# Moving all query and key projections of a hybrid encoder step ahead of its linear attention, by way of a DRAM scratch

## The chip, the core and the metric

The kernel runs on one core of a Trainium2 chip. A core has TensorE (PE in the profile; its weight loads are listed apart as PEld), VectorE (DVE), ScalarE (ACT), GpSimd (POOL) and SyncE (SP), which here issues every DMA. The metric is the device time of one execution in microseconds, as the median of several runs.

## What is computed

The reference is one layer of an encoder step, for a prompt of 1024 frames (8 tiles of 128) and 32 sample frames of a running stream. All arithmetic is fp32.

```
xn = rmsnorm(x);  u = xn @ w_in            # 1024 x (11 groups of columns)
gq, gk, gv, gr, gg, dq, dk, dv, dg, ma, mb = split(u)
dq, dk = rope(dq), rope(dk)                # first 16 of every 64 channels
o_gla  = gated linear attention, 4 heads, chunk by chunk (a running state)
for each of 8 heads of differential attention:
    p1 = softmax(q1 k1^T / 8), p2 = softmax(q2 k2^T / 8)   # block-causal mask
    o_diff = (p1 - lam * p2) @ v
merged = sigmoid(ma) * (yg @ w_proj_gla) + sigmoid(mb) * (yd @ w_proj_diff)
y = x + rmsnorm(merged @ w_out)            # yg, yd: normed, times silu(gg), silu(dg)
```

The rotated keys and the values are outputs as well. The sample's 32 frames attend to 512 cached keys and to themselves.

## The kernel before

Every fp32 matrix product is done as three products of split operands: a rounded high part and the rest, high x high, low x high, high x low. So each weight tile and each activation has a high and a low half, made by a copy on ACT and a subtraction on DVE or POOL.

A **projection block** is one 128-column slice of a weight matrix against all 1056 frames: 3 chunks of 352 frames x 8 slices of the inner dimension x 3 products = 72 matmuls. `wtile` (line 422) loads its 512 KB of weights, rounds them on ACT (line 426) and subtracts on POOL (line 428). `proj` (line 431) runs a block in one go; `fill` (line 441) runs a list of blocks in pieces of two inner slices, to be woven between other work.

The stages, in order:

1. normalisation of the input, and the values of both attentions (lines 326 to 415);
2. gated linear attention (GLA, lines 481 to 752): per head `gla_prep` makes the decay factors and the scaled q and k, `gla_head` walks over nine chunks with a running state;
3. differential attention (lines 754 to 1048): `diff_main` takes eight heads one behind the other, and in each head eight query blocks; `sample_thread` does the sample frames;
4. the output projections of GLA (`pg_first`), of the differential heads, and the final product with `w_out`.

In stages 2 and 3 the order of PE's instructions is written out by a planner, the class `Order` (line 62). It keeps a modelled clock, the banks of PSUM in use and a table `W` of assumed latencies. Several generators offer their next step with a cost and the events that it needs; the planner takes the first one in the list that is ready. The attention threads stand first, the projection blocks of `fill` last, so blocks go where the attention threads are waiting by the plan. The other engines are ordered by the scheduler of the language, with a higher priority for `diff_main`. PE then executes its instructions in this fixed order, whatever the real latencies are.

The list of blocks decides what there is to weave in. In stage 2 it is, head after head, two silu gate blocks of the head before, q and k, and then as many **gate blocks** (the sigmoid gates ma and mb, 16 in all, stored to DRAM) as `GATES_GLA` says: [0, 1, 1, 1, 1]. A silu block of head h needs head h-1 to be finished, a q block the previous head's `if`, a k block the previous head's transposed keys. In stage 3 each head h has the rotated query block and the rotated key block of head h+1, its own silu block `dgate_job` (which needs the end of head h-1), and gate blocks by `GATES_DIFF`: [2, 1, 1, 1, 1, 1, 1, 2, 2], the first entry ahead of head 0. The names "dq", "dk" in `W` are the latencies that the planner assumes from the end of such a block to usable operands.

The rotated blocks are where the change lies. `rot_job` (line 784) evacuates a block into `rr` (line 799), swaps eight rows at a time by four small DMAs into `sw` (lines 791 and 792), multiplies `sw` with the sines on POOL (line 793), multiplies and adds on DVE (lines 795 and 797), and calls `split_q` (line 802) or `split_k` (line 818). These write the high and low halves of the two sub-heads; for matmuls over 128 rows each sub-head's 64 rows must stand twice, and for the keys four DMAs copy 64 rows to the other 64 (line 832). The key tiles k0, k1, kl0, kl1 have one buffer each, the query tiles two.

`diff_main` (line 895) emits, for a head, the scores of block 0 (`diff_scores`, line 864), the closing steps of the previous head (`diff_fin`), the load of the head's values into a buffer `sg1` (line 903), which in stage 2 held the silu gate, and then for each i the scores of block i+1, the transposes of block i (line 926) and, after every second block, the product with the values (lines 939 to 941). The scores of the next head come behind all this.

## Time and profile before

| | |
|---|---|
| median of 3 runs | 1517.67 us (1513.35 to 1520.35) |
| the profiled execution | 1523.35 us, span 1521.6 us |
| mean granted TensorE clock | 0.981 |
| DMA | 152.29 MB, mean 100 GB/s |
| stage 2 on PE | about 222 to 551 us |
| first scores of differential attention | 601.8 us |
| first output projection | 1220.7 us |

The profile is of one execution. Per group of instructions it gives the source line, engine, operation, tiles, count, busy time, mean duration, and the idle time of the engine just before them with what ended it. PE's matmuls are pipelined: the duration of one (some 320 ns for 352 columns) is longer than the distance to the next (some 160 ns), so for PE the useful measure is how many start in a stretch. Further views are the chain of waits that ended last, the waits, the busy time by stretch of time and the timeline.

### The profile page before, as it was taken

The page shows a single profiled execution, that of the slowest core. Times are in us where ns is not written, and L with a number is a line of the kernel's source. Part 1 is how long each engine was busy: PE and PEld are TensorE (multiplying, and loading weights), DVE is VectorE, ACT ScalarE, POOL GpSimd, SP SyncE. Part 2 cuts the span into 40 slices and gives each one's busy share as a digit, 9 for nine tenths or more (in the row PEclk, how much of TensorE's full clock was granted, in tenths as well). Part 3 has the DMA queues.
Part 4 walks back from the last instruction along what each step waited for, and adds up shares of the span by engine and source line. Part 5 has one row for each costly group of instructions (what it writes and reads, how often), then busy time and mean ns, then how long its engine had stood idle before and what let it go on. Part 6 is the DMA issues. An engine that isn't in the chain of part 4 may idle for free.

```text
span 1521.6 us, 22330 instructions
## 1 busy us (share of the span) xinstructions
PE 1438.6 (95%) x8848; PEld 1340.6 (88%) x8848; DVE 792.0 (52%) x1464; ACT 623.2 (41%) x1282; POOL 298.4 (20%) x186
## 2 busy tenths in 40 slices
PE   8999999989999998998999998989899999999997
PEld 6787789889989898998989897989798889999997
DVE  5602005655474343757685866677764544155415
ACT  4603114635353323564655564555555443022311
POOL 1200002222222233121222222212221112122001
PEclk9999999999999999999999998999999999999999
DMA  8621111221222144131323132223212187433305
GB/s 294 205 104 37 44 48 43 61 85 56 89 70 78 58 145 130 46 88 60 102 75 88 60 102 76 74 73 88 89 50 89 67 271 248 168 130 117 109 1 187
DMA packets 66118, 152.29 MB, mean 100 GB/s; under 512 B 9920, under 2 KB 28480, under 8 KB 65488
## 3 DMA queue, kind: packets, MB, share of 16 engines
q1 hardware_dynamic: 66000, 150.71, 30.9%
q8 instruction: 74, 1.21, 0.3%
q14 instruction: 44, 0.36, 0.1%
HBM read 100.16 MB, written 39.98 MB: 92 GB/s over the span
## 4 chain that ended last, share of the span: by engine, by line
PE 51%; DVE 7%; ACT 4%; DMA 2%; issue 1%; POOL 1%; SPq 0%; DVEq 0%; POOLq 0%; ACTq 0%
PE ps_w L458 9%; PE ps_w L459 9%; PE ps_w L460 9%; PE ps_w L437 2%; PE ps_w L436 2%; PE ps_w L438 2%; PE ps_c L1176 2%; PE ps_c L1174 2%; PE ps_c L1175 2%; PE ps_t L926 2%; PE ps_s L879 2%; PE ps_s L878 2%; DVE p L888 1%; DMA kl<-kl 1%; PE po L940 1%
## 5 line engine op out<-in xcount | busy, mean ns | idle before, releaser
L458 PE MATMUL ps_w<-X,wh 128*128 128x352 f32 x1344 | 455.2, 339 | 7.5 <-ACT k L489 3.2
L459 PE MATMUL ps_w<-X,wl 128*128 128x352 f32 x1344 | 440.2, 328 | 0.0
L460 PE MATMUL ps_w<-X,wh 128*128 128x352 f32 x1344 | 438.3, 326 | 0.0
L428 POOL TENSOR_TENSOR wl<-wr,wh 128x1024 fp32r<-128x1024 f32 x72 | 178.5, 2479 | 688.5 <-ACT wh L426 551.2
L458 PEld LDWEIGHTS ps_w<-X,wh 128*128 128x128 f32 x1344 | 257.9, 192 | 12.5 <-DVE sg L471 4.0
L459 PEld LDWEIGHTS ps_w<-X,wl 128*128 128x128 f32 x1344 | 257.9, 192 | 1.2 <-issue 1.2
L460 PEld LDWEIGHTS ps_w<-X,wh 128*128 128x128 f32 x1344 | 258.5, 192 | 0.0
L884 ACT ACTIVATE p<-ps_s,nm 128x256 f32<-128x256 f32 (+7 forms) x128 | 94.4, 740 | 60.8 <-DVE nm L882 35.9
L426 ACT ACTIVATE wh<-wr 128x1024 fp32r<-128x1024 f32 x72 | 75.9, 1054 | 61.0 <-PE ps_w L460 35.7
L283 PE MATMUL ps_v<-wh,X 128*128 128x512 f32 x248 | 97.6, 394 | 1.4 <-DVE X L222 1.4
L282 PE MATMUL ps_v<-wh,X 128*128 128x512 f32 x248 | 98.3, 397 | 0.0
L284 PE MATMUL ps_v<-wl,X 128*128 128x512 f32 x248 | 98.2, 396 | 0.0
L882 DVE TENSOR_REDUCE nm<-ps_s 128x1 f32<-128x256 f32 (+7 forms) x128 | 95.0, 746 | 2.7
L880 DVE MEMSET ps_s<- 64x64 f32 x128 | 14.3, 112 | 118.4 <-PE ps_s L879 116.9
L269 DVE TENSOR_TENSOR vo<-ps_v,vo 32x512 f32<-32x512 f32 x4 | 2.7, 679 | 140.7 <-ACT vo L268 140.7
L926 PE MATMUL ps_t<-ident,p 128*128 128x128 f32 x288 | 49.0, 280 | 25.6 <-DVE ps_s L880 13.8
L928 ACT ACTIVATE ah<-ps_t 128x512 fp32r<-128x512 f32 (+2 forms) x96 | 46.8, 488 | 58.5 <-PE ps_t L926 57.8
L878 PE MATMUL ps_s<-k,q 128*128 128x512 f32 (+2 forms) x192 | 69.3, 368 | 1.2 <-DMA k<-k 1.2
L879 PE MATMUL ps_s<-kl,q 128*128 128x512 f32 (+2 forms) x192 | 65.0, 354 | 4.0 <-DMA kl<-kl 3.8
L643 POOL TENSOR_TENSOR vl<-vr,vh 128x512 fp32r<-128x512 f32 (+1 forms) x20 | 24.8, 1238 | 223.2 <-ACT vh L642 223.2
L265 ACT ACTIVATE vo<-ps_v 128x512 f32<-128x512 f32 x32 | 19.0, 595 | 114.9 <-PE ps_v L284 114.5
L926 PEld LDWEIGHTS ps_t<-ident,p 128*128 128x128 f32 x288 | 35.9, 143 | 32.8 <-issue 22.5
(318 smaller groups left out, 3039.3 us busy)
## 6 DMA issues: line engine op xcount, KB each, us to landing
wr<-w SPq DMA_DIRECT2D x72, 512.0 KB
thd<-gate SPq DMA_DIRECT2D x16, 528.0 KB
xn<-xn SPq DMA_DIRECT2D x16, 512.0 KB
wr<-wv SPq DMA_DIRECT2D x16, 512.0 KB
newk<-rr SPq DMA_DIRECT2D x8, 528.0 KB
ygr<-ygd SPq DMA_DIRECT2D x8, 528.0 KB
tha<-thd SPq DMA_DIRECT2D x8, 528.0 KB
ydr<-ydd SPq DMA_DIRECT2D x8, 528.0 KB
```

What stands on the lines that cost most here:

```text
L282: mm(ps, xk[:, 0, t0 : t0 + P], wh[:, k, :], start=(k == 0), stop=False)
L283: mm(ps, xk[:, 1, t0 : t0 + P], wh[:, k, :], start=False, stop=False)
L284: mm(ps, xk[:, 0, t0 : t0 + P], wl[:, k, :], start=False, stop=(k == KT - 1))
L428: nc.gpsimd.tensor_tensor(wl, wr, wh.bitcast(F32), op=ALU.subtract)
L458: mm(ps[:, :n], wh[:, k, :], src[k][:, 0, t0 : t0 + n], start=(k == 0), stop=False)
L459: mm(ps[:, :n], wl[:, k, :], src[k][:, 0, t0 : t0 + n], start=False, stop=False)
L460: mm(ps[:, :n], wh[:, k, :], src[k][:, 1, t0 : t0 + n], start=False, stop=(k == KT - 1))
L878: mm(ps[:, n0 : n0 + n], qs[m][:, qsl], ks[m][:, n0 : n0 + n], start=True, stop=False)
L879: mm(ps[:, n0 : n0 + n], qs[m][:, qsl], kls[m][:, n0 : n0 + n], start=False, stop=True)
L882: ve.tensor_reduce(nm, ps[:, 0:w], axis=AX.X, op=ALU.max, negate=True)
L884: act(p[:, 0:w], ps[:, 0:w], AF.Exp, bias=nm, accum_out=sm[:, m : m + 1])
L926: nc.tensor.transpose(ps[:, (j - j0) * P : (j - j0 + 1) * P], p[:, j * P : j * P + P], ident)
```

## The change

All 16 query and key blocks of differential attention, and two gate blocks, run in a dense stage of their own, behind the values and before GLA. Their raw results go to two flat DRAM scratch tensors `qd` and `kd`, the queries already scaled. Rotation is done for four heads at a time: the 8 + 8 rotated rows of four heads' sub-heads are gathered from the scratch into one 128-row tile, turned there by three DVE operations and stored back. GLA has no gate blocks any more; differential attention has 14 gate blocks and no rotated blocks. Each head's operands are loaded from the scratch in `diff_main` of the head before, at query blocks 1, 3 and 5: each sub-head's rows are loaded twice and then split in place. Keys have two buffers. Weights of the new stage have three raw buffers.

```diff
-GATES_GLA = [0, 1, 1, 1, 1]
-GATES_DIFF = [2, 1, 1, 1, 1, 1, 1, 2, 2]
+GATES_GLA = [0, 0, 0, 0, 0]
+GATES_DIFF = [2, 2, 2, 2, 2, 1, 1, 1, 1]
-N = {"fin": 1, "rr": 3, "q": 2, "k": 4, "fill": 2, "first": 200, "evac": 1200, "lead": 2}
+N = {"fin": 1, "rr": 3, "q": 2, "k": 2, "fill": 2, "first": 200, "evac": 1200, "lead": 2}
...
-    "dq": 7.76, "dk": 14.32,
+    "dq": 16.0, "dk": 16.0,
...
+    qd = dram.tile([D, T], F32, name="qd")
+    kd = dram.tile([D, T], F32, name="kd")
...
+    def turn(d, g, new):
+        part = lambda s: d.rearrange("(a c) t -> a c t", c=HD)[g * 8 : g * 8 + 8, s * 8 : s * 8 + 8, :]
+        r = rq.tile([P, T], F32, tag="r", name="r")
+        sw = rq.tile([P, T], F32, tag="sw", name="sw")
+        for s in range(2):
+            dma(r[s * HD : s * HD + HD], part(s))
+            dma(sw[s * HD : s * HD + HD], part(1 - s))
+        ve.tensor_tensor(sw, sw, stb, op=ALU.mult)
+        ve.tensor_tensor(r, r, ct, op=ALU.mult)
+        ve.tensor_tensor(r, r, sw, op=ALU.add)
+        for s in range(2):
+            st(part(s), r[s * HD : s * HD + HD])
+            if new is not None:
+                for h in range(4):
+                    o = r[s * HD + h * 16 : s * HD + h * 16 + 16]
+                    st(new[4 * g + h].rearrange("(m d) t -> m d t", m=2)[:, s * 8 : s * 8 + 8, :], o)
+
+    def qk_block(b, d, h, scale, new):
+        r = rq.tile([P, T], F32, tag="nat", bufs=3, name="nat")
+        proj(wtile(b + h, rq, 3), xs, lambda ps, sl: act(r[:, sl], ps, AF.Copy, scale=scale))
+        st(d[h * P : h * P + P], r)
+        if new is not None:
+            for m in range(2):
+                st(new[h, m * HD + 16 : m * HD + HD, :], r[m * HD + 16 : m * HD + HD])
+    late = ()
+    for g in range(2):
+        for b, d, scale, new in ((BLK_DK, kd, 1.0, a["newk"]), (BLK_DQ, qd, SC, None)):
+            for h in range(4 * g, 4 * g + 4):
+                qk_block(b, d, h, scale, new)
+                if h == 4 * g and late:
+                    turn(*late)
+            late = d, g, new
+    for n in range(2):
+        b, event, begin, _ = gate_job(*gates.pop(0))
+        evac, done = begin()
+        proj(wtile(b, rq, 3), xs, evac)
+        done()
+        if n == 0:
+            turn(*late)
+    rq.release()
...
+    def fetch_rows(t, d, h, m):
+        for half in (0, HD):
+            dma(t[half : half + HD], d[(2 * h + m) * HD : (2 * h + m + 1) * HD, 0:NP])
+    def fetch_k(h):
+        kls = [dp.tile([P, NP], F32R, tag=f"kl{m}", bufs=2, name=f"kl{m}") for m in range(2)]
+        for m in range(2):
+            fetch_rows(kls[m].bitcast(F32), kd, h, m)
...
+    def split_k(h):
+        for m in range(2):
+            kl = dks[h][1][m]
+            kh = dp.tile([P, NP], F32R, tag=f"k{m}", bufs=2, name=f"k{m}")
+            for c in parts(NP, N["k"]):
+                act(kh[:, c], kl[:, c].bitcast(F32), AF.Copy)
+                ve.tensor_tensor(kl[:, c], kl[:, c].bitcast(F32), kh[:, c].bitcast(F32), op=ALU.subtract)
...
+    def fetch_q(h, m):
+        raw = tp.tile([P, NP], F32, tag="sg1", name="qraw")
+        fetch_rows(raw, qd, h, m)
+        return raw
+    def split_q(h, m, raw):
+        q = dp.tile([P, NP], F32R, tag=f"q{m}", bufs=2, name=f"q{m}")
+        for c in parts(NP, N["q"]):
+            act(q[:, c], raw[:, c], AF.Copy)
+            ve.tensor_tensor(q[64:128, c], raw[64:128, c], q[64:128, c].bitcast(F32), op=ALU.subtract)
...
+    def head_ahead(h, i, raw):
+        if i == 1:
+            fetch_k(h)
+            return fetch_q(h, 0)
+        if i == 3:
+            split_k(h)
+            split_q(h, 0, raw)
+            return fetch_q(h, 1)
+        if i == 5:
+            split_q(h, 1, raw)
+            return fetch_v(h)
+        return raw
...
+                if h + 1 < DH:
+                    raw = head_ahead(h + 1, i, raw)
                 if i + 1 < NQ:
                     yield from diff_scores(h, i + 1, att)
...
+    raw0 = None
+    for i in (1, 3, 5):
+        raw0 = head_ahead(0, i, raw0)
```

Removed are `rot_job`, the old `split_q` and `split_k`, their rope tables and swap tile, and the load of the values at the start of a head.

## The prediction

> **What bounds the kernel now.** I read the page first: its busy shares.

> ```profile
> span 1521.6 us, 22330 instructions
> PE 1438.6 (95%) x8848; PEld 1340.6 (88%) x8848; DVE 792.0 (52%) x1464; ACT 623.2 (41%) x1282; POOL 298.4 (20%) x186
> ```

> PE is busy 95% of the span, no other engine more than 52%. So time can leave only through PE's holes, or through less matmul work. The change removes no matmul. It moves whole projection blocks between stages, so the question is where PE will have something to do. Next I asked for the busy time by stretch (columns: window, length, busy us and count of PE, PEld, DVE, ACT, POOL, clock, DMA share, GB/s): gated linear attention (GLA), the wait for the first head, and the eight heads.

> ```profile
> 222.00:550.00 328.00, 306.31 (x1981) 293.12 (x1980) 177.94 (x298) 140.64 (x277) 83.84 (x51) 0.99 0.23 70
> 550.00:600.00 50.00, 49.56 (x315) 48.97 (x314) 20.48 (x33) 17.22 (x36) 16.81 (x8) 1.00 0.41 132
> 600.00:1220.00 620.00, 580.79 (x3632) 546.52 (x3630) 411.65 (x790) 325.94 (x718) 141.04 (x66) 0.97 0.27 80
> ```

> GLA leaves PE idle 328 - 306.3 = 21.7 us, the heads 620 - 580.8 = 39.2 us. The same stretches for the matmul of line 458 alone, of which a projection block has 24, and the dense stage of line 436, where blocks follow each other with nothing between:

> ```profile
> 222.00:550.00 328.00, 160.76 (x487) 92.11 (x487) 0.99 0.23 70
> 550.00:600.00 50.00, 31.10 (x98) 18.22 (x97) 1.00 0.41 132
> 600.00:1220.00 620.00, 263.30 (x761) 147.56 (x760) 0.97 0.27 80
> L436 PE MATMUL ps_w<-Y,wh x192: 317/322/329, 1323.4 to 1415.5; 128*128 128x352 f32 x192
> ```

> Eight blocks start within 92.1 us, so a block is 11.5 us of PE. GLA held 487/24 = 20.3 blocks, the 50 us 4.1, the heads 31.7. In GLA blocks are 233 of 328 us; in the heads 365 of 620. The rest is the stage's own chain with its holes: 95 us in GLA, 255 us (32 a head) in the heads. The blocks are what covers those chains.

> **The change part by part.**

> *The new dense stage.* 16 query/key blocks and 2 gates: 18 x 11.5 = 207 us. By the shapes in the diff, a block loads 0.5 MB of weights and stores 0.5 MB, a key another 0.4 MB, and a turn moves about 2 MB: some 30 MB in 207 us, 145 GB/s. The 50 us stretch above carried 132 GB/s at a DMA share of 0.41, so DMA is half used. Prices on ACT, POOL and SP:

> ```profile
> L426 ACT ACTIVATE wh<-wr 128x1024 fp32r<-128x1024 f32 x72 | 75.9, 1054 | 61.0 <-PE ps_w L460 35.7 <-PE ps_w L438 13.6 <-PE ps_w L1095 8.6
> L428 POOL TENSOR_TENSOR wl<-wr,wh 128x1024 fp32r<-128x1024 f32 x72 | 178.5, 2479 | 688.5 <-ACT wh L426 551.2 <-PE ps_t L926 58.9 <-ACTq L572 37.4
> L477 SPq DMA_DIRECT2D thd<-gate x16: 319/332/424, 333.4 to 1210.5; - x16
> ```

> ACT 1.05 + 3 evacuations of 0.46 (a row of the next part) = 2.4 us, POOL 2.5 us, SP some five issues of 0.33 us: all far inside 11.5 us. The four turns (four heads in one tile, three DVE operations on 1056 columns) lie beside later blocks, the last one beside the gates. The second gate reuses the first one's only buffer, so its evacuation waits for a store, with a second PSUM bank as cover. I add 3 us for this and the stage's edges (bounds 0 and 10). **+210 us.**

> *GLA loses its four gates* (one each behind k1, k2, k3 and the last silu). If they were pure load, that is -46 us. I followed the third GLA head (ACT and DVE timelines; start, length):

> ```profile
> 400.03 0.46 ACT L489 ACTIVATE k<-ps_w 128x352 f32<-128x352 f32 x1 [1.73 <-PE ps_w L460]
> ...
> 416.02 0.47 ACT L477 ACTIVATE gate<-ps_w 128x352 f32<-128x352 f32 x1 [6.06 <-PE ps_w L460]
> ...
> 423.40 0.44 ACT L470 ACTIVATE sg<-ps_w 128x352 f32<-128x352 f32 x1
> ...
> 428.64 0.60 ACT L628 ACTIVATE kdh<-ps_kt 128x512 fp32r<-128x512 f32 x1
> ```

> ```profile
> 408.51 0.75 DVE L715 SCALAR_TENSOR_TENSOR yt<-ps_y,gg_half,sg 128x512 f32<-128x512 f32 x1 [2.68 <-DMA ygd<-yt]
> ```

> The key projection ends at 400.0. The next job, a silu block, must wait for the previous head's last output, written at 408.5 (L715). The gate fills just this hole: silu could start some 8 to 10 us earlier, not 16. And the chain from the key's evacuation to the transposed keys (400.0 to 428.6, 28.6 us) does not shorten at all when a gate disappears. So a gate gives back its time only partly. Behind k1 the hole ends with the first head's output and nothing is gained. Behind k2 and k3 the next projections come that much earlier, but the chain of the same head does not. Behind the last silu the fourth head's chain runs alone (DVE timeline):

> ```profile
> 527.59 0.52 DVE L471 SCALAR_TENSOR_TENSOR sg<-sg,ps_w 128x352 f32<-128x352 f32 x1 [1.41 <-ACT sg L470]
> ...
> 551.50 0.48 DVE L680 SCALAR_TENSOR_TENSOR s_new<-s_new,eb,pS 128x256 f32<-128x256 f32 x1 [0.87 <-PE pS L674]
> ...
> 562.62 0.75 DVE L715 SCALAR_TENSOR_TENSOR yt<-ps_y,gg_half,sg 128x512 f32<-128x512 f32 x1 [4.18 <-DMA ygd<-yt]
> ```

> From the last silu (528.1) to the last state (551.5) is 23.4 us, in which a gate now fills PE; that gate's removal leaves a hole and saves nothing. One step of about 10 us (k2's, carried to the end), 2 us from k1's and 4 us because chunks no longer wait behind whole pairs of filler matmuls: **-16 us** (bounds -10 and -46).

> *The heads lose 14 blocks* (16 rotation blocks out, two gates in: 36 to 22). With the rest of the stage as it is, from 551.5 to the first output projection,

> ```profile
> L1093 PE MATMUL ps_w<-y,wh x48: 319/323/1282, 1220.7 to 1248.7; 128*128 128x352 f32 x48
> ```

> 669 us in all, 14 blocks are -161 us. Now what this does to the rest. Off DVE go:

> ```profile
> L795 DVE TENSOR_TENSOR rr<-rr,ct 128x352 f32<-128x352 f32 x48 | 29.4, 634 | 17.4 <-DMA sw<-rr 17.4
> L797 DVE TENSOR_TENSOR rr<-rr,sw 128x352 f32<-128x352 f32 x48 | 23.3, 510 | 0.0
> L829 DVE TENSOR_TENSOR kl<-rr,k 64x256 fp32r<-64x256 f32 x32 | 15.7, 491 | 0.9
> L811 DVE SCALAR_TENSOR_TENSOR q<-rr,q 64x512 fp32r<-64x512 f32 x16 | 14.8, 924 | 0.5
> L257 DVE TENSOR_TENSOR wl<-wr,wh 128x1024 fp32r<-128x1024 f32 x16 | 19.4, 1220 | 4.1 <-ACT wh L255 4.1
> L793 POOL TENSOR_TENSOR sw<-sw,stb 128x1056 f32<-128x1056 f32 x16 | 40.9, 2554 | 16.2 <-DMA sw<-rr 13.0 <-DVE sg L471 1.9 <-DVE sm L887 1.3
> ```

> 52.7 us of rotation and about twice 15.7 + 14.8 us of splits (each has a twin line of the same shape): 114 us, 14 a head. On come four half-width subtractions each for keys and queries, 8 x 0.61 (half of L257's 1.22) = 4.9 us a head. Net -9 us of DVE a head, and POOL's 41 us go. That helps only where DVE is last: L926's holes, in

> ```profile
> L926 PE MATMUL ps_t<-ident,p 128*128 128x128 f32 x288 | 49.0, 280 | 25.6 <-DVE ps_s L880 13.8 <-DVE sm L887 5.3 <-DVE al L929 4.1
> ```

> are 25.6 us in all; I credit 10. Against it stands the drain between heads. The last scores of head 0 and the first of head 1, on PE:

> ```profile
> 654.67 0.44 PE L878 MATMUL ps_s<-k,q 128*128 128x512 f32 x1
> ...
> 674.53 0.27 PE L878 MATMUL ps_s<-k,q 128*128 128x128 f32 x1
> ```

> 19.9 us pass, because diff_main emits the next head only behind the softmax, the transposes and the value product of the last block. The change does not alter that order; loads two blocks ahead are hidden either way, and the second key buffer saves a copy wait, not this chain. It is filled by blocks now, 4 a head. Then there are three (heads 0 to 3) or two (4 to 7), and the silu block among them needs the previous head's end. The planned start of head 0, 16 us behind GLA, is too early as well: its raw query shares the buffer sg1 with the last silu, read at 562.6, 11 us behind GLA's last state; then come two loads in series, each like a head's key copy (chain of waits):

> ```profile
> 600.54 4.77 DMA kl<-kl
> ```

> 11 + 2 x 4.8 + two splits of 1.2 = 23 us against 16: 7 to 8 us of hole, which the 10 above roughly cancel. Moved off SP are 64 row swaps and 32 key copies, 0.33 us each, on come 10 issues a head; a query load behind its split holds up the weight loads behind it on SP by a microsecond or two, which have a block's time. **-160 us** (bounds: -200, if all 39 us of holes went; -130, if the four two-block heads each leave 8 us more of the drain open).

> **Sum:** 1521.6 + 210 - 16 - 160 = 1556 us of span. The profiled run took 1523.35 us, 1.75 over its span, and 5.7 over the median of 1517.67; so 1556 + 1.75 - 5.7 = **1552 us**, 2.3% slower.

> **A clock rule beside it.** A hole on PE, and the granted clock (third number from the end) in the stretch before it and its own:

> ```profile
> 689.70 0.41 PE L926 MATMUL ps_t<-ident,p 128*128 128x128 f32 x2 [2.79 <-DVE ps_s L880]
> ```

> ```profile
> 640.00:680.00 40.00, 40.00 (x260) 38.79 (x259) 24.97 (x49) 22.30 (x47) 10.51 (x5) 1.00 0.27 75
> 680.00:720.00 40.00, 35.28 (x204) 33.57 (x203) 28.66 (x52) 20.74 (x46) 7.34 (x3) 0.91 0.20 66
> ```

> 0.09 x 40 = 3.6 us of clock lost in a stretch with this hole. If the drains add two such holes a head, up to 16 x 1.8 = 29 us follow wherever PE is the bound; I leave it out of the sum, since PE is seldom the bound behind a drain. [...]

> **The rivals.**

> *Faster: rotation was the trouble.* If the 9 us of DVE a head and the POOL work were what made PE late, all 39 us of the heads' holes go (-200) and GLA gives 25: 1521.6 + 210 - 25 - 200 = 1507, at the median 1503. For it: DVE ends most of L926's holes. Against: the biggest share is named as waiting on the softmax itself, and blocks no longer cover it. It decides once GLA and heads together give back more than 217 us. Chance 0.20.

> *No change: GLA really gives its four gates back* (-46) and the heads -160: 1525.6, at the median 1522. Against: the 28.6 and 23.4 us chains. Chance 0.10.

> *Much slower: the two-block heads become bound by softmax and drain*, with splits queued on DVE and ACT ahead of it: heads -130, GLA -10: 1591, at the median 1588. For it: 32 + 2 x 11.5 = 55 us a head against 411.65/8 - 9 = 42 us of DVE. Chance 0.12.

> The forecast has 0.58.

> **How the numbers follow.** 0.5% (7.6 us) is about what a measurement here can tell from no change: below 1510 is faster, above 1525 slower. Faster 0.20, same 0.10, slower 0.58 + 0.12 = 0.70. The range goes from the faster rival's 1503 to the slow one's 1588, which cuts about half of each off; rounded 1504 to 1588. Both signs are in it; the forecast's own range is 1530 to 1575.

> **What would show it.** Right: a dense stretch of about 208 us behind the value projections with PE full; GLA about 312 us long with PE busy near 83% ((306.3 - 46)/312); in the heads more PE idle in total than 39 us, mostly before L926's transposes and between two heads; heads near 66 us, then near 55. Wrong: GLA under 295 us, or last state to first output projection under 475 us instead of 509, or a hole in the dense stage at weights or evacuations.

## The result, and the profile after

The changed kernel takes 1668.5 us (median of 4 runs, 1661.88 to 1673.6) against 1517.93 us: ratio 1.0993, 95% interval 1.0946 to 1.104. It is 150 us slower, where the prediction said 34 and at most 70. The profiled execution is the slowest of the four (1673.6 us), and those of the experiments lie up to 7 us to either side of their medians. So a difference of less than some ten microseconds between the stages of two single profiles is not read as a gain or a loss below.

The page after: the span, the busy shares, and two of its rows by 40 slices (tenths: PE busy, granted clock).

```profile
span 1671.6 us, 22195 instructions
PE 1493.8 (89%) x8848; PEld 1381.4 (83%) x8848; DVE 724.9 (43%) x1348; ACT 611.3 (37%) x1234; POOL 254.6 (15%) x169
PE   8999969999998798787798898987977869999998
PEclk9999979999999899987899899988979879999999
```

PE runs the same 8848 matmuls, and its busy time grew by 55 us: the same work, partly at a lower clock (mean 0.930, before 0.981). Its idle time grew from 83 to 178 us. VectorE fell by 67 us, as the change intended, and this bought nothing.

Now by stage. Three marks cut the run: the end of the value projections, the last state of linear attention (GLA) and the first output projection. The last two after:

```profile
773.85 0.48 DVE L737 SCALAR_TENSOR_TENSOR s_new<-s_new,eb,pS 128x256 f32<-128x256 f32 x1 [1.81 <-PE pS L731]
```

```profile
L1142 PE MATMUL ps_w<-y,wh x48: 318/323/733, 1371.9 to 1399.7; 128*128 128x352 f32 x48
```

Busy time by stretch (window, length, busy us and count of PE, PEld, DVE, ACT, POOL, clock, DMA share, GB/s), before: GLA, heads.

```profile
222.10:552.00 329.90, 308.21 (x1996) 294.94 (x1995) 178.92 (x301) 141.29 (x279) 83.84 (x51) 0.99 0.23 71
552.00:1220.70 668.70, 628.34 (x3930) 593.56 (x3928) 431.17 (x821) 343.20 (x751) 157.85 (x74) 0.97 0.28 84
```

After: the new dense stage, GLA, heads.

```profile
218.30:445.60 227.30, 211.19 (x1299) 210.58 (x1299) 23.44 (x16) 44.59 (x76) 47.52 (x20) 0.96 0.46 138
445.60:774.30 328.70, 282.06 (x1728) 266.72 (x1726) 172.56 (x297) 132.26 (x263) 76.08 (x47) 0.92 0.20 61
774.30:1371.90 597.60, 499.46 (x2899) 451.65 (x2899) 347.90 (x694) 297.53 (x644) 80.01 (x43) 0.88 0.29 84
```

The value projections end 3.8 us earlier, the dense stage adds 227.3, GLA gives back 1.2, the heads 71.1, what follows 1.2: together +150.0, the whole difference of the spans. In the heads PE's busy time fell by 128.9, not by the 161 of 14 blocks, and its idle time rose from 40.4 to 98.1. So 90 us that the heads should have given are 58 us of holes and 32 us of slower matmuls.

The dense stage opens with a hole. PE (start, length, and in brackets the idle time before and what ended it), then SP's queue:

```profile
218.14 0.32 PE L564 MATMUL ps_z<-gst,a2s 96*128 96x352 f32 x1
233.08 0.95 PE L439 MATMUL ps_w<-X,wh 128*128 128x352 f32 x2 [14.63 <-ACT wh L429]
235.52 0.66 PE L440 MATMUL ps_w<-X,wl 128*128 128x352 f32 x1 [1.48 <-POOL wl L431]
```

```profile
219.71 0.33 SPq L273 DMA_DIRECT2D newv<-vo  x1
220.13 0.61 SPq L490 DMA_DIRECT2D ct<-ropec  x1
220.79 1.37 SPq L492 DMA_DIRECT2D stb<-ropes  x2
222.21 1.39 SPq L427 DMA_DIRECT2D wr<-w  x3
```

The first weights (L427) stand on SP behind the last store of the values and the three rope loads. They are issued 4 us after PE went idle and take 11 more to be usable.

In the heads the waits of PE (us in total, times, longest) now read:

```profile
PE ps_t L977 <- DVE al L980: 26.7, 16, 2.1
PE ps_s L927 <- DVE q L863: 11.6, 2, 5.9
PE ps_t L977 <- DVE p L938: 11.1, 6, 3.0
```

The first was 4.1 us before: transposes that wait until VectorE has evicted the low half of the group before. The second is the late query of head 0.

### The profile page after: what moved, and what is told of

Its sections match the earlier page's. It is cut to its first block, busy times and chain, and to the rows that moved or that the text cites. A ratio compares the mean times of both kernels' runs of the same rounds, so it can differ in the third digit from the quotient of the medians.

```text
span 1671.6 us, 22195 instructions
## 1 busy us (share of the span) xinstructions
PE 1493.8 (89%) x8848; PEld 1381.4 (83%) x8848; DVE 724.9 (43%) x1348; ACT 611.3 (37%) x1234; POOL 254.6 (15%) x169
## 4 chain that ended last, share of the span: by engine, by line
PE 38%; DVE 5%; ACT 5%; DMA 3%; issue 1%; SPq 0%; POOL 0%; DVEq 0%; POOLq 0%; ACTq 0%
PE ps_w L461 5%; PE ps_w L462 5%; PE ps_w L463 5%; PE ps_t L977 2%; PE ps_w L440 2%; PE ps_w L439 2%; PE ps_w L441 2%; PE ps_c L1225 2%; PE ps_c L1223 2%; PE ps_c L1224 2%; PE ps_s L927 2%; PE ps_s L928 2%; ACT p L933 1%; PE po L991 1%; PE po L990 1%; PE po L992 1%
## 5 line engine op out<-in xcount | busy, mean ns | idle before, releaser
L287 PE MATMUL ps_v<-wl,X 128*128 128x512 f32 x248 | 98.1, 396 | 0.0
L285 PE MATMUL ps_v<-wh,X 128*128 128x512 f32 x248 | 98.1, 395 | 0.0
L977 PE MATMUL ps_t<-ident,p 128*128 128x128 f32 x288 | 56.3, 311 | 44.5 <-DVE al L980 26.7
L931 DVE TENSOR_REDUCE nm<-ps_s 128x1 f32<-128x256 f32 (+7 forms) x128 | 94.1, 747 | 2.8
L502 DVE TENSOR_TENSOR r<-r,ct 128x1056 f32<-128x1056 f32 x4 | 8.1, 2028 | 198.8 <-DMA r<-kd 117.3
L977 PEld LDWEIGHTS ps_t<-ident,p 128*128 128x128 f32 x288 | 38.5, 157 | 57.1 <-DVE al L980 33.4
```

The source lines that it names most:

```text
L285: mm(ps, xk[:, 0, t0 : t0 + P], wh[:, k, :], start=(k == 0), stop=False)
L287: mm(ps, xk[:, 0, t0 : t0 + P], wl[:, k, :], start=False, stop=(k == KT - 1))
L977: nc.tensor.transpose(ps[:, (j - j0) * P : (j - j0 + 1) * P], p[:, j * P : j * P + P], ident)
```

## The experiments

All 18 runs: the median, and from each profile the time from the end of the values to the last state (with the dense stage, where there is one), and from there to the first output projection ("heads").

| | median us | to last state | heads |
|---|---|---|---|
| before | 1517.9 | 329.9 | 668.7 |
| after | 1668.5 | 556.0 | 597.6 |
| e1 before, no GLA gates | 1521.2 | 334.3 | 668.3 |
| e2 before, 10 head gates less | 1517.4 | 330.4 | 666.1 |
| e3 after, 14 blocks more | 1749.0 | 557.8 | 669.4 |
| e4 after, one operand set | 1648.3 | 556.2 | 574.6 |
| e5 after, first weights early | 1648.5 | 535.6 | 588.3 |
| e6 after, 4 gates to GLA | 1659.3 | 559.0 | 584.5 |
| e7 after, gates held | 1659.9 | 555.2 | 587.1 |
| e8 after, small matmuls | 1694.3 | 556.5 | 614.1 |
| e9 after, no head gates | 1615.5 | 553.2 | 543.4 |
| e10 e5, e6, e7 together | 1631.9 | 545.5 | 566.8 |
| e11 after, no row maximum | 1664.1 | 554.3 | 580.6 |
| e12 before, no row maximum | 1506.3 | 334.1 | 653.1 |
| e13 after, scores ahead | 1672.5 | 553.9 | 594.4 |
| e14 after, two banks | 1642.7 | 556.1 | 558.5 |
| e15 e10 and scores ahead | 1634.8 | 544.3 | 563.5 |
| e16 before, two banks | 1573.7 | 328.9 | 714.7 |
| e17 e10 and two banks | 1616.1 | 543.1 | 553.1 |
| e18 e3 and two banks | 1742.9 | 555.1 | 659.7 |

e1 to e4 and e9 are single timed runs, so only tens of microseconds are read from their medians. The numbers in brackets behind other medians are the ratio to the kernel before, timed beside it, and its 95% interval; by these intervals a gain of 9 us over the changed kernel (1.0993, 1.0946 to 1.104) stands just clear of the noise. e1, e2, e4, e9, e11 and e12 leave work out, so their times are probes and no gains. Some expectations count the heads from another mark, the last output of GLA, to the last product with the values: 583.5 us in the changed kernel, and by that mark 528.3 in e9, 581.3 in e13, 545.3 in e14 and 646.8 in e18. Theory 1: blocks were cover for chains of latency, and with fewer of them the chains show. Theory 2: the new operand path (loads, splits) holds the heads up. Theory 3: the holes cost the clock, and the clock costs the time.

### What a block is worth, and the operand path (e1 to e4)

**e1**

```diff
-GATES_GLA = [0, 1, 1, 1, 1]
+GATES_GLA = [0, 0, 0, 0, 0]
```

> The kernel before, with the four gate blocks of the linear-attention stage left out (their outputs are read from the gates of other blocks): 4 x 11.5 = 46 us of TensorE work less in that stage, nothing else moved. Theory 1 (fill starvation: the stage is paced by its own chain of vector and scalar work, and the gates ran in its holes for nothing): the stage stays at 329 us within 8, the run at 1510 to 1520 us. The forecast's rate (a block is worth something there, 16 us for the four): the stage at about 313, the run near 1502. A stage bound by TensorE gives back 46: run near 1472.

GLA without its four gates:

```profile
219.10:553.40 334.30, 284.38 (x1730) 268.85 (x1728) 175.40 (x301) 131.76 (x263) 74.97 (x47) 0.91 0.19 57
```

Four blocks less, and not a microsecond gained (334.3 against 329.9; the run 1521.2 beside 1521.4 of the kernel before). PE's busy time fell by 24 us instead of 46, with the clock at 0.91 instead of 0.99: what was left ran slower, in the time that the chain needs anyway. In GLA a gate was worth nothing.

**e2**

```diff
-GATES_DIFF = [2, 1, 1, 1, 1, 1, 1, 2, 2]
+GATES_DIFF = [2, 0, 0, 0, 0, 0, 0, 0, 0]
...
+        if h >= 0:
+            jobs.append(dgate_job(h))
         if h + 1 < DH:
             jobs.append(rot_job(BLK_DK + h + 1, ("dk", h + 1), need, split_k(h + 1)))
-        if h >= 0:
-            jobs.append(dgate_job(h))
```

> The kernel before, with ten of the twelve gate blocks of the softmax heads left out (their outputs are read from other gates), and the head's own gate block set between the query and the key block of the next head: 26 blocks in the heads instead of 36, with the old operand path. Theory 1 (a block in the heads is partly cover and its removal gives back only what the changed kernel showed, 74 us for 14 blocks, 5.3 each): heads 669 to about 616 us, run near 1463. Theory 2 (a block is worth its 11.5 us and the new operand path of the changed kernel, loads and splits, ate the rest): heads near 554, run near 1402.

Ten blocks less, heads 2.6 us shorter: both theories missed. The waits name why this run can't price a block: a new wait of the fill itself heads the list.

```profile
PE ps_w L458 <- ACT rr L799: 31.2, 5, 8.3
PE ps_t L926 <- DVE al L929: 24.7, 13, 2.9
```

With the gates gone, rotated blocks follow each other more closely and wait for their one buffer `rr`. The second line is the wait that the changed kernel shows too, here with the old operand path. That speaks against theory 2; for the price the run is inconclusive.

**e3**

```diff
+        if 0 <= h and h + 1 < DH:
+            jobs.append(more_job(BLK_DQ + h + 1, need))
...
+        if 0 <= h and h + 1 < DH:
+            jobs.append(more_job(BLK_DK + h + 1, need))
```

> The changed kernel with fourteen more projection blocks in the fill of the heads (weights loaded and split, 72 matmuls, evacuated, result not stored): two a head, with the needs that the query and key blocks had, so that the heads hold 36 blocks as before but with the new operand path. Theory 1 (starvation): the blocks fall into holes, the heads come back to what they took before, 595 to about 669 us, +74, run near 1742. Theory 2 (the operand path costs the missing 86 us): 595 + 161 = 756, run near 1830. A third case, heads bound by something that blocks do not touch: under +40, run under 1710.

```profile
776.80:1446.20 669.40, 620.08 (x3906) 583.62 (x3906) 368.77 (x693) 343.05 (x712) 115.21 (x57) 0.97 0.29 86
```

Theory 1: the 14 blocks cost 71.8 us where it said 74, and with 36 blocks the heads take 669.4 us, as before the change (668.7); that the two agree to a microsecond is luck. PE's idle time is back at 49 us and the clock at 0.97. A block cost 5.1 us of the 11.5 that it takes on PE. So under full cover the new operand path is no dearer than the old one.

**e4**

```diff
+        if h:
+            if i == 3:
+                dks[h], qsam[h], ksam[h] = dks[0], qsam[0], ksam[0]
...
+            if i == 5:
+                dqs[h] = dqs[0]
...
+                return fetch_v(h)
+            return raw
```

> The changed kernel with heads 1 to 7 using the split query and key operands of head 0: no query or key loads, no splits on ScalarE and VectorE after the first head; value loads, softmax, matmuls and fill as they were. Theory 1 (starvation): the operand path is not what the heads wait for, heads 595 within 20, run 1648 to 1675. Theory 2 (operand path): the heads lose most of the missing 86 us, run under 1610.

The heads lose 23.0 us, a little more than the 20 that theory 1 allowed, and the run 20. That is what seven heads' loads and splits cost here (38 us of VectorE and 30 of ScalarE less in the heads), a quarter of the missing 90. Theory 2 falls as the main cause.

### Repairs one by one (e5 to e8, e10)

**e5**

```diff
+            if u == 3 and i == 1:
+                w_raw = wp.tile([P, KT, P], F32, tag="wr", bufs=1, name="wr")
+                dma(w_raw, a["w128"][BLK_DK])
+            if u == 3 and i == 5:
+                w_first = wtile(None, w_raw)
...
+                if g == 0 and b == BLK_DK and h == 2:
+                    dma(ct, a["ropec"][0:8].unsqueeze(0).to_broadcast([16, 8, T]))
...
```

> The changed kernel with the weights of the first block of the new dense stage loaded and split during the last value pass, and the loads of the rope tables set behind the third block. Theory: the 14.63 us hole at the head of that stage and the half clock behind it (17 us, up to 8.5 lost) come from the SP queue, on which the first weights stand behind the value stores and the rope loads; the stage should fall from 220 us to about 202, the run by 16 to 24, to about 1648. Rival: the stores and loads themselves are what is slow there (the second block's weights come late in the place of the first): run within 8 us of 1668.

The run is 20 us faster (ratio 1.0861, 1.0811 to 1.091), and the stretch up to the last state 20.4 us shorter. From the end of the values on, PE is busy without a gap, at full clock:

```profile
217.80:420.00 202.20, 202.20 (x1260) 202.20 (x1259) 22.01 (x13) 41.98 (x71) 43.42 (x18) 1.00 0.48 148
```

So the two gaps (14.63 + 1.48 us) and the matmuls at half clock around the second one (5.1 us of busy time from 233.08 to 239.68, clock 0.50; an estimated 2.5 us lost) came from the place of the first load: 4 us in the queue, and 11 us of loading and splitting with nothing for PE to run meanwhile. The rest of the stage was not slow. The edit also moves the rope loads back; what that alone gives was not tried.

**e6**

```diff
-GATES_GLA = [0, 0, 0, 0, 0]
-GATES_DIFF = [2, 2, 2, 2, 2, 1, 1, 1, 1]
+GATES_GLA = [0, 1, 1, 1, 1]
+GATES_DIFF = [2, 2, 1, 1, 1, 1, 1, 1, 0]
```

> The changed kernel with four of the gate blocks put back into the linear-attention stage, where the kernel before had them, and taken out of the heads (10 gates there instead of 14). Theory 1 (a block is free in linear attention, holds the clock there, and is worth 5.2 us in a head): linear attention 342 (from the last value to its last output, 218.3 to 783.8 less the 220 of the dense stage) unchanged or up to 6 less, heads -21, run near 1645. Forecast's rule (11.5 us a block in a head, 4 in linear attention): heads -46, linear attention +16, run near 1638. A block worth nothing in a head at this count: run within 6 of 1668.

9 us faster (1.0912, 1.0855 to 1.097). GLA takes the four blocks for 3.0 us in all, which is no more than two profiles can differ by; its clock is back at 0.99:

```profile
445.80:777.50 331.70, 308.86 (x1995) 295.94 (x1994) 174.46 (x297) 140.89 (x277) 85.07 (x51) 0.99 0.24 74
```

The heads give 13.1 us for 46 us of work, less than expected, and their clock falls to 0.85.

**e7**

```diff
-GATES_DIFF = [2, 2, 2, 2, 2, 1, 1, 1, 1]
+GATES_DIFF = [0, 2, 2, 2, 2, 2, 2, 2, 0]
...
+        for held in range(n):
+            b, event, begin, _ = gate_job(*gates.pop(0))
+            jobs.append((b, event, begin, [(("qk", h), 0.0)] if held else []))
```

> The changed kernel with two gate blocks for each of heads 0 to 6, the second held back until the head's last scores are issued, so that it runs in the drain of the head; same work. Theory 1 with its detail (the gates run ahead, and the drains have nothing left to fill them): TensorE's idle time in the heads, 89.6 us, falls below 60, run 1630 to 1655. Rival (it is the number of blocks, not their place): idle and run within 10 us of the changed kernel.

The rival: 9 us faster (1.0919, 1.0872 to 1.0966), and PE idle in the heads for 93 us instead of 98.

```profile
773.50:1360.60 587.10, 493.96 (x2899) 443.95 (x2899) 345.42 (x693) 298.10 (x646) 79.84 (x43) 0.89 0.29 86
```

At the same number of blocks their place matters little.

**e8**

```diff
+    def warm_thread():
+        while True:
+            yield 0.45, [], ["pj"]
+            ps = bank("ps_warm")
+            for _ in range(2):
+                mm(ps[:, 0:P], one_h, one_h, start=True, stop=True)
...
```

> The changed kernel with small matmuls that compute nothing (pairs of 128x128) wherever the planned order of the heads had no step ready; nothing else moved. Theory 3 (34 us of the heads' 86 are matmuls at half clock, which the holes bring on): half-clock time in the heads falls from 135 us to under 80, run 1640 to 1655. If the clock is only a by-product and the chain paces the heads anyway: half-clock time falls, run within 8 us of 1668; if the small matmuls delay the chain, slower.

26 us slower. The clock came back (0.97) and more than half of the idle time went (39 us are left of 98), yet the heads are 16.5 us longer:

```profile
776.40:1390.60 614.20, 575.25 (x3950) 543.31 (x3950) 359.42 (x690) 294.98 (x640) 79.53 (x42) 0.97 0.28 82
```

PE's busy time rose by 76 us: the 1072 small matmuls are work as well. That they delayed the chain that they stood beside fits this, but no run shows it apart. So the run shows that a full clock alone doesn't save the heads; how much of the 32 us of slower matmuls would come back by itself stays open. Theory 3 is not borne out as the main cause.

**e10**, the edits of e5, e6 and e7 in one kernel.

> The changed kernel with the three edits together that each gave a little: first weights loaded during the value pass, four gates in linear attention, the last gate of each head held back for its drain. If they add up (20, 9 and 9 us alone): 1668 - 38, near 1630. If two of them fill the same holes: 1640 to 1650. In no case near the kernel before, 1520.

They add up: 1631.9 us (1.0737, 1.0715 to 1.0758), 37 us for 20 + 9 + 9.

### Which chain paces the heads (e9, e11 to e18)

**e9**

```diff
-GATES_DIFF = [2, 2, 2, 2, 2, 1, 1, 1, 1]
+GATES_DIFF = [0, 0, 0, 0, 0, 0, 0, 0, 0]
...
```

> The changed kernel with all fourteen gate blocks left out of the heads (their outputs are read from the two gates of the dense stage), so that a head's fill is its own gate block alone: 161 us of TensorE work less. Theory 1 (at 22 blocks the heads already run at the pace of their own chain): from the last output of linear attention to the last weighted sum of values 583.5 to 545 to 560 us, 25 to 40 less, run 1630 to 1645. The forecast's constant (32 us a head of own chain and holes, about 12 us a block): some 160 less, heads near 423, run near 1510.

```profile
771.80:1315.30 543.50, 373.93 (x1891) 309.41 (x1891) 336.84 (x694) 267.57 (x590) 45.66 (x29) 0.79 0.23 65
```

Theory 1 in kind, with more gained than it said (55 us where it had 25 to 40: 528.3 by its own mark, 545 to 560 expected), and far from the 423 of the forecast's constant. With one block a head the heads still take 543.4 us, 68 each; PE is idle for 170 us of it, and the clock is at 0.79. From 8 to 22 blocks one costs 3.9 us, from 22 to 36 it costs 5.1: nowhere in this range does PE alone set the pace. The leading waits:

```profile
PE ps_t L977 <- DVE al L980: 54.9, 32, 2.7
PE ps_t L977 <- DVE p L938: 25.2, 12, 3.4
```

**e11 and e12**, the same cut in both kernels:

```diff
-            ve.tensor_reduce(nm, ps[:, 0:w], axis=AX.X, op=ALU.max, negate=True)
-            act(p[:, 0:w], ps[:, 0:w], AF.Exp, bias=nm, ...)
+            act(p[:, 0:w], ps[:, 0:w], AF.Exp, bias=zero, ...)
```

> The changed kernel without the row maximum of the softmax (the exponential takes a zero bias instead): 128 VectorE reductions, 94.1 us at 747 ns, leave the chain from scores to exponential; TensorE's work is the same. Theory 1 (the chain paces the heads after the change): the heads lose 25 to 60 us, run 1610 to 1645. If TensorE or the queue order paces them: under 12, run 1656 to 1668.

> The same cut in the kernel before (95.0 us of reductions leave the chain of its heads). Theory 1 (there the fill covers the chain and TensorE is the bound): under 15 us, run 1505 to 1521, clearly less than the changed kernel gets from the same cut. If the chain paces both alike: the same 25 to 60 as in the changed kernel.

In the profiles the heads are 17.0 us shorter after and 15.6 before, for some 95 us of VectorE each time. But the profiled executions of the changed kernel and of e11 are 15 us apart, their medians only 4: 1664.1 (1.0956, 1.0897 to 1.1014), within the noise of the changed kernel. The kernel before gets 14 us shorter (1506.3 against 1520.1 beside it; 0.9911, 0.9887 to 0.9934). Theory 1 as put here misses: the changed kernel was to get 25 to 60, and clearly more than the kernel before. The row maximum is mostly hidden in both and is not the link.

**e13**

```diff
                 if i + 1 < NQ:
                     yield from diff_scores(h, i + 1, att)
+                elif h + 1 < DH:
...
+                    yield from diff_scores(h + 1, 0, ahead)
                 p, lat = att.pop(i)
```

> The changed kernel with the first scores of the next head issued before the last block of a head is transposed, which the two buffers of keys and queries allow; all else in the same order, same work. If the seam between heads is what the fill used to cover (from the last scores of a head to the first of the next now 14 to 25 us): 7 seams at 6 to 12 us, heads 583.5 to 500 to 540, run 1585 to 1625. If the holes lie inside the heads (one bank for transposes): run within 10 us of 1668.

1672.5 us (1.1015, 1.0978 to 1.1053): nothing. But the edit only moves the seam. Here are heads 6 and 7: the stretch from the last scores of one to the first of the next, and from there to the scores of its second block; two rows of the kernel before, two of the changed one, two of e13.

```profile
1126.46:1144.22 17.76, 17.76 (x123) 17.70 (x122) 12.83 (x26) 10.27 (x21) 2.86 (x2) 1.00 0.39 110
1144.22:1150.95 6.73, 6.15 (x34) 5.10 (x34) 2.19 (x7) 4.84 (x10) 2.42 (x1) 1.00 0.08 27
1286.69:1301.23 14.54, 8.01 (x40) 7.16 (x38) 6.49 (x10) 4.36 (x8) 0.00 (x0) 0.65 0.00 0
1301.23:1306.74 5.51, 2.84 (x9) 1.35 (x10) 2.38 (x7) 4.27 (x9) 2.38 (x1) 0.81 0.00 0
1286.70:1289.58 2.88, 0.75 (x9) 0.51 (x6) 2.48 (x4) 2.40 (x4) 0.00 (x0) 1.00 0.00 0
1289.58:1306.69 17.11, 10.28 (x44) 8.09 (x41) 5.51 (x13) 6.45 (x14) 2.36 (x1) 0.66 0.00 0
```

In e13 the first scores come after 2.9 us instead of 14.5, but the second ones after 20.0, as in the changed kernel (20.1): the transposes and the value product of the last block now stand behind the first scores. Over all seven seams, these two stretches together last 170 us before the change, 164 after it, 167 in e13 and 154 in e9. So the drain of a head takes 22 to 24 us, with 36, 22 or 8 blocks to fill it (in e3, where more fill stands ahead of the second scores, it takes 32). PE is idle in it for 3 us before the change, 49 after it, 52 in e13 and 70 in e9. Of the 58 us of new holes, 46 lie here. e13 doesn't shorten the drain and so can't say what a shorter one would give.

**e14**

```diff
+                    tag, nt = ("t", "pj")[nt % 2], nt + 1
-                    ps = tbank("ps_t")
+                    ps = (tbank if tag == "t" else bank)("ps_t")
```

> The changed kernel with the transposes of the heads alternating between their own bank and the fill's two, so that a group can be transposed while the one before is evicted; same work. If the single bank is the link (TensorE waits 26.7 us there in the run of the changed kernel, ahead of L977 on VectorE's low half): heads 583.5 to 555 to 565, run 1640 to 1655. If the fill loses as much by sharing its banks: within 10 us of 1668.

26 us faster (1.0819, 1.0785 to 1.0853). In the profiles, whose executions are 35 us apart, the heads are 39.1 us shorter, PE is idle for 84.5 us instead of 98.1, and the clock is at 0.93 instead of 0.88. So 13.6 of the 39.1 us are holes, and 25.4 are the same matmuls in less busy time:

```profile
775.50:1334.10 558.60, 474.06 (x2877) 432.55 (x2877) 352.21 (x689) 297.47 (x643) 82.92 (x42) 0.93 0.31 90
```

This is one link of the chain, the largest single one found. It acts in the drain: the seven drains last 145 us instead of 164, and PE is idle in them for 27 us instead of 49. One turn of the bank in the changed kernel, on PE, ScalarE and VectorE:

```profile
1016.05 0.63 PE L977 MATMUL ps_t<-ident,p 128*128 128x128 f32 x4 [0.86 <-DVE p L938]
1018.09 1.12 PE L977 MATMUL ps_t<-ident,p 128*128 128x128 f32 x4 [1.41 <-DVE al L980]
```

```profile
1016.72 0.60 ACT L979 ACTIVATE ah<-ps_t 128x512 fp32r<-128x512 f32 x1
```

```profile
1017.35 0.69 DVE L980 TENSOR_TENSOR al<-ps_t,ah 128x512 fp32r<-128x512 f32 x1 [0.23 <-ACT ah L979]
```

Four transposes, their high half copied, their low half subtracted, and only then the next four into the same bank: 2.04 us a turn, with 0.63 of PE's work in it. The heads have 96 evictions, half of them with fewer than four transposes; at 2 us each, an upper estimate from this one turn, that is some 190 us in which PE has use for other work, 24 us a head. The bank is not the whole chain: with two of them the first of PE's waits is for the softmax ahead of the transposes (11.1 us in the changed kernel).

```profile
PE ps_t L979 <- DVE p L938: 26.5, 9, 5.4
```

**e15**, e10 with the edit of e13.

> The kernel with the three edits of the run at 1632 us, and the first scores of the next head ahead of the last block of a head as well. If the seam is what paces the heads at 18 blocks: another 50 to 80 us, run 1550 to 1580, still slower than the kernel before (1520), since the dense stage of 206 us remains. If not: within 12 us of 1632.

1634.8 us (1.0784, 1.0736 to 1.0832), as e10: moving the seam gives nothing at 18 blocks either.

**e16 and e17**, the edit of e14 in the kernel before, and in e10.

> The kernel before with the transposes of the heads alternating between their own bank and the fill's two. If the bank is a link only where fill is thin: TensorE waited 4.1 us there on VectorE's low half in the kernel before against 26.7 us in the changed one, so at most 0 to 8 us, run 1512 to 1520 (and up to 10 us slower if the 36 blocks of fill lose by sharing). If it paces the heads whatever the fill: another 38 us, run near 1481.

> The kernel of the run at 1632 us (first weights early, four gates in linear attention, last gate of a head held back) with the transposes on two banks as well. If the bank is what paces heads with 18 blocks: 35 to 55 us less, run 1577 to 1597. If the held gates had already covered that wait: 1615 to 1632. Either way slower than the kernel before.

e16 is 57 us slower (1.0363, 1.0338 to 1.0389), outside both figures. Its waits are no longer at the transposes but at the sample's product and at keys that arrive late:

```profile
PE po_s L1016 <- DVE smp L1006: 22.5, 3, 7.5
PE ps_s L878 <- DMA k<-k: 20.6, 5, 8.1
PE ps_s L879 <- DMA kl<-kl: 13.0, 10, 2.4
```

With other banks the planner writes another order; that it is the single key buffers of that kernel which don't bear it fits these waits, but was not tried apart. e17 is 16 us faster than e10 (1616.1, 1.0658, 1.0622 to 1.0693), about what the second case named: the held gates cover part of the same wait. No version with the whole work beats the kernel before.

**e18**, e3 with two banks, to tell e16's loss from the effect of full cover.

> The changed kernel with fourteen more blocks in the fill of the heads (as in the run at 1749 us, results not stored) and the transposes on two banks. If the bank is a link only where fill is thin: TensorE, busy 615 of 656 us there, has little left to gain, heads 645 to 665, run 1740 to 1760. If it is a link at any fill and the loss in the kernel before came from its late keys: heads near 620, run near 1712.

1742.9 us (1.1476, 1.1444 to 1.1509), 6 less than e3; the heads 9.7 us shorter, against 39.1 with 22 blocks. So the bank is a link mainly where fill is thin. With two banks the step from 22 to 36 blocks costs 101.2 us, 7.2 a block instead of 5.1: the looser the chain, the nearer a block comes to its 11.5 us.

## Why the prediction was wrong

The direction and the kind of cause were right: work was moved out of places where it was cover into a stage where it costs its full time. The prices of the cover were wrong, all to the same side: 17 us too little for the dense stage, 15 and 89 too much for what GLA and the heads would give back.

- **Dense stage, +210, measured 227.3.** The 207 us of blocks and the cheapness of the four turns held (e5). The edge was taken as 3 us, bounded by 10; it was 20. The step that failed counted SP's issues per block. It did not ask what stands ahead of the first one (the values' last store and the rope loads, 4 us), nor what PE does until the first weights are loaded and split (nothing, for 11 us). The prediction had named a hole at the weights as a sign that it was wrong.
- **GLA, -16, measured -1.2.** The step "k2's, carried to the end" had no ground: e1, where the four gates alone were left out, gains nothing. That agrees with the chains that the prediction quoted itself (28.6 and 23.4 us). Its bounds, -10 to -46, left out nothing gained at all.
- **Heads, -160, measured -71.1.** This is the step that failed by most of the error: "With the rest of the stage as it is", 32 us a head of own chain and holes. That residual had been measured under 36 blocks of cover and belongs to them. e9 shows the heads at 68 us each with one block, where the same rule gives 32 + 11.5 = 43.5. Of the missing 90 us, e4 ties up to 23 to loads and splits, and e14 26 (by the medians) to 39 (by the profiles) to the one bank of the transposes. The two may overlap. So at least 28 us of the 90 stay open: no run here says which part of the chain they belong to.
- **The 10 us credited to VectorE's relief.** VectorE lost 83 us in the heads (431.2 to 347.9), and PE's idle time rose. Part of what PE waits for there is VectorE's place in a chain with one bank (e14), not its load; e4, with 38 us of VectorE and 30 of ScalarE less again, gave 23.
- **The start of head 0**, 7 to 8 us of hole: 11.6 measured. The step had the wait right and was 4 us short.
- **The drain between heads** stands in the sum at nothing and in the bound at 30 us (-130 instead of -160); it was the reason for the worst case (1588). The place was right and the price too small: 46 us more of holes lie there, between all heads and not only the two-block ones, and matmuls at a lower clock beside them (0.65 in the row of 1286.69).
- **The clock**, priced at up to 29 us and left out of the sum. 32 us of slower matmuls were measured in the heads (clock 0.88, before 0.97). Whether they set the end, e8 doesn't settle; in e14, 25 us of PE's busy time went together with 14 us of holes.
- **Rivals.** "Rotation was the trouble" asked for 217 us from GLA and heads together; they gave 72. "GLA gives its gates back" is refuted by e1. The much slower case had the place right, softmax and drain, and the size too small (-130 for the heads). Its check could not show it: 42 us of VectorE a head is a load, and the 68 us of a head with one block are made of latencies that no engine's busy share shows.
- **The range** ended at 1588 because its three terms were bounded by less than they could lose; the bound for a block in the heads stopped at 130 of 161 us, while in GLA the same paragraph had already found blocks that give back nearly nothing.

## What to carry to other kernels

A block of matmuls that is woven into a stage is worth what the stage gets shorter without it, not its duration: here 11.5 us of work was worth 0 in GLA and 4 to 5 in the heads, while in a stage of its own it cost all 11.5. Before work is taken out of a stage at 94% PE, leave some of it out and time that; the stage's own chain can't be had by subtracting the work from the total. Look for the drain between two rounds, which takes its time however little fills it (22 to 24 us a head here), and for a buffer that is used one turn at a time: its turns (2 us here) show when the cover goes. And when an edit moves a wait, look whether the stretch behind it got longer before calling the wait harmless.

## What the runs showed of the hardware

In the changed kernel the granted clock fell behind holes even shorter than the 2.79 us one of the prediction. Two stretches of 3.41 us in its heads, around the turn quoted above (the clock is the third number from the end):

```profile
1014.54:1017.95 3.41, 1.28 (x9) 0.77 (x7) 3.17 (x5) 2.93 (x6) 1.23 (x1) 1.00 0.39 159
1017.95:1021.36 3.41, 3.27 (x16) 3.27 (x17) 3.13 (x4) 1.00 (x2) 1.37 (x1) 0.50 0.29 59
```

The gaps are 0.86 and 1.41 us long; PE is busy for 1.28 of 3.41 us, and the whole next stretch ran at half clock (0.50) although PE was busy in 3.27 of it. In GLA one gap of 1.86 us went with the same:

```profile
628.82:632.24 3.42, 3.42 (x24) 3.42 (x22) 0.88 (x1) 0.47 (x1) 0.00 (x0) 1.00 0.59 171
632.24:635.65 3.41, 1.55 (x14) 1.28 (x12) 1.18 (x2) 0.00 (x0) 0.00 (x0) 1.00 0.32 120
635.65:639.06 3.41, 3.41 (x14) 3.41 (x14) 0.69 (x1) 0.00 (x0) 0.00 (x0) 0.50 0.06 21
```

```profile
222.20:239.30 17.10, 4.73 (x15) 4.28 (x16) 0.00 (x0) 2.12 (x2) 4.68 (x2) 0.51 0.77 187
239.30:256.40 17.10, 17.10 (x107) 17.10 (x106) 0.00 (x0) 2.81 (x5) 2.40 (x1) 0.99 0.34 114
```
